# Up projections of two squared-ReLU MLPs: seven products of operand quarters in place of eight, in a one-core transformer kernel

## The chip, the cores and the metric

The kernel runs on 1 core of one Trainium2 chip. The metric is the device time of one execution in microseconds (us), as the median of several runs; lower is better. The core has TensorE (PE, matrix products; PEld is its weight load), VectorE (DVE), ScalarE (ACT), GpSimd (POOL) and SyncE (SP, which here only issues DMAs).

## The reference

Two transformer stacks over 512 tokens of width 1024, all in fp32. The first is one layer with attention, a memory cross-attention and a SwiGLU MLP. The second has two layers, each a mixer (mLSTM in the first, latent attention in the second) and then the MLP with which the change deals:

```python
ada = cond @ ada_w[l] + ada_b[l]                      # shift, scale and gate rows
sh1, sc1, g1, sh2, sc2, g2 = split(ada, 6)
x = x + g1 * rmsnorm(mixer(modulate(rmsnorm(x, norm_g[l, 0]), sh1, sc1)), norm_g[l, 1])
h = modulate(rmsnorm(x, norm_g[l, 2]), sh2, sc2)
y = square(relu(h @ mlp_w1[l])) @ mlp_w2[l]           # [512,1024] @ [1024,4096], @ [4096,1024]
x = x + g2 * rmsnorm(y, norm_g[l, 3])
```

## The kernel before

Every fp32 operand is held as two parts of 12 significant bits (`hi`, `lo`, type fp32r), and every product is three matmuls: hi by hi (L361), hi by lo (L362), lo by hi (L363), summed in PSUM (`ps`).

Weights stream from DRAM in chunks of 512 KB into `raw` (three buffers; L335 on SP's queue). A chunk is split into two parts, in pieces of 128x512: ACT copies the high part (L260), DVE subtracts it from the chunk for the low part (L261). Split chunks lie in the pool `s8` (14 buffers), which also holds the activations' parts. How many chunks may be split ahead is a cap (`w0` ... `w7`, `lc`). Where a weight has a gain by row, L270 and L271 do the same with the gain. `parts` (L481 ACT, L482 DVE) splits activations in the same way.

A squared-ReLU MLP has 4096 hidden columns, 32 hidden tiles of 128. They are worked in blocks (`mb`: 8, 6, 6, 6, 6 tiles). In a block, two tiles (a pair, 256 columns) at a time are made: per pair 2 tiles x 8 k-tiles x 3 = 48 matmuls of 128x512, then per tile a ReLU from PSUM on ACT (L1281), a square on DVE (L1283) and the split (L481, L482). Of the first block, the first two pairs (`fp`) are worked in two halves of 256 tokens, so that they can start while the layer's input is still being made. Then the block's down projection: for each half of the output columns and each of four token tiles the products over all k of the block in one bank; the first block is copied to an accumulator on ACT (L1184), later ones are added to it on DVE (L1186). The last block's down projection is woven with the step to the next layer (`boundary`).

A background generator (`ada`, `row_by`) makes the modulation rows of later layers: DVE multiplies a chunk of 256 KB of `ada_w` by a column of `cond` and adds it to an accumulator (L700, scalar_tensor_tensor 128x512). The chunks come by SP's queue (L704) into the tile `araw`, which has two buffers. A step is issued for each `pace` of matmul work; the steps run through the first of the two MLPs and end in the mixer behind it, so that the second MLP has none.

The kernel's instructions are written by generators and then put in order by a scheduler; each engine works its list strictly in that order. The list is fixed when the program is built.

The lines of the after kernel lie about 152 higher: L261 becomes L308, L482 L634, L700 L852, L704 L856, L1186 L1343, L361 to L363 L445 to L447.

Of the kernel before, what the change touches and what calls it, by code (L numbers as in the profile page):

```python
# [10 lines left out]
F32 = mybir.dt.float32  # L11
# [4 lines left out]
ALU = mybir.AluOpType  # L16
# [17 lines left out]
BUF = dict(s8=14, u2=16, row=3, raw=3, w0=4, w1=4, w2=4, w3=5, w4=5, w5=5, w6=5, w7=7, ps=8, pace=3, pacb=2.5, man=0, lag=3, lagx=3, lagm=3, half=1, quiet=1, xp=0, fp=2, r1=1.25, r1b=3.6, r1c=2.4, r2=1.6, r2b=2.6, rx=1.4, rm=0.6, pre=10, gl=3, pl=0, hb=300, hs=0, ha=0, sp=0, spq=1.3, sq=1, b1=1, b2=1, lc=7, mb=(8, 6, 6, 6, 6), mb2=(8, 6, 6, 6, 6), st2=1, pr2=8, z1=4.5, z2=5, gt=3, rv=2, gs=1, rl=3, n1=4, ex=2, em=3, vg=1, sb=(8, 8, 6), mo=4, x1=2, g0=20, st=1, y1=0, y2=1, y3=0, ph=2, pq=0, fy=1, u1=6, s32=4, sm=60)  # L34
# [19 lines left out]
class Nothing:  # L54
    """Stands for the core and its tiles while the order of the weights is drawn up."""
# [11 lines left out]
class HT:  # L67
    """A transposed operand [128, nk, ntok] as two exact parts, in tiles made when first used."""
# [36 lines left out]
class Net:  # L105
    def __init__(self, tc, args, out, dbg=None, specs=None, pools=None):
# [10 lines left out]
        self.n_lo = self.n_load = self.n_ready = self.n_take = 0  # L117
# [51 lines left out]
    def pump(self):  # L169
        """Loads and splits as far ahead as there is room for, in the order of use."""  # L170
# [3 lines left out]
        while more:  # L174
            more = False
            if self.n_load < len(self.specs) and self.raw_live < BUF["raw"]:
                i = self.n_load
                kk, cc, loader = self.specs[i][:3]
                self.raws[i] = self.t("raw", [P, kk, cc], F32, BUF["raw"])
                for f in self.before.pop(i, ()):  # L180
                    f()
                loader(self, self.raws[i])
                self.n_load += 1
                self.raw_live += 1
                more = True
            if self.n_ready < self.n_load:
# [13 lines left out]
    def piece(self):  # L200
        i, last, f = self.pieces.pop(0)
        f()
        if last:
            self.raw_live -= 1
            self.pump()
# [1598 lines left out]
```

## Time and profile before

| | |
|---|---|
| median of 3 runs | 2011.02 us (2007.4, 2011.02, 2011.51) |
| profiled execution, span | 2008.3 us |
| PE busy | 1961.0 us (98%) |
| DVE busy | 1256.9 us (63%) |
| ACT busy | 922.5 us (46%) |
| POOL busy | 311.5 us (16%) |

The profiled execution's own time is given by its span alone, and lies 2.7 us under the median. Busy shares are averages over stages. The first MLP's stretch from its sixth hidden tile to its last runs from 1112 to 1408 us of the span, the second's from 1672 to 1973 us.

### The profile page before, as it was taken

How to read it: one execution, taken by the hardware profiler on the slowest of the kernel's cores; microseconds unless marked ns; L12 is line 12 of the kernel's file. 1: busy time of each engine (PE TensorE's matmuls, PEld its weight loads, DVE VectorE, ACT ScalarE, POOL GpSimd, SP SyncE). 2: the span in 40 equal slices, each digit the busy share in tenths (PEclk: the TensorE clock that was granted, in tenths of full speed). 3: DMA queues.
4: the chain of work that ended last, by engine and by line, in shares of the span. 5: the costliest groups of instructions: out<-in, count | busy, mean ns of one | idle time of the engine just before them, and what ended most of it. 6: DMA issues, size and time to landing. Idle time of an engine off the chain costs nothing.

```text
span 2008.3 us, 27160 instructions
## 1 busy us (share of the span) xinstructions
PE 1961.0 (98%) x9652; PEld 1631.0 (81%) x9652; DVE 1256.9 (63%) x2379; ACT 922.5 (46%) x2073; POOL 311.5 (16%) x599
## 2 busy tenths in 40 slices
PE   8999999999999999999998999999999989999998
PEld 6888988878888888778887888888788878888886
DVE  5756655757558585757768557677777573444444
ACT  7767774645344243436534343233556543422331
POOL 1421113013100000511116000000420060000000
PEclk9999999999999999989999999999999999999999
DMA  6322342434446464244333455555341221422321
GB/s 209 92 80 77 114 136 64 143 100 126 148 152 206 138 213 139 69 136 140 118 116 108 144 163 184 169 185 177 111 132 43 85 74 53 128 95 93 95 84 42
DMA packets 191655, 244.98 MB, mean 122 GB/s; under 512 B 20059, under 2 KB 119488, under 8 KB 191520
## 3 DMA queue, kind: packets, MB, share of 16 engines
q1 hardware_dynamic: 185264, 232.15, 37.3%
q0 software_dynamic: 6256, 11.10, 2.1%
q8 instruction: 76, 1.25, 0.3%
q14 instruction: 59, 0.48, 0.1%
HBM read 241.00 MB, written 2.20 MB: 121 GB/s over the span
## 4 chain that ended last, share of the span: by engine, by line
PE 89%; DVE 6%; ACT 2%; issue 1%; DMA 1%; POOL 1%; SPq 0%; POOLq 0%; DVEq 0%; ACTq 0%
PE ps L361 26%; PE ps L362 26%; PE ps L363 26%; PE ps L859 1%; DVE s L271 1%; DVE x L502 1%; PE ps L1637 1%; DVE s L261 1%; PE ps L1666 1%; PE ps L1397 1%; PE ps L830 1%; PE ps L474 1%; PE ps L843 1%; PE ps L1143 1%; DVE s L482 1%
## 5 line engine op out<-in xcount | busy, mean ns | idle before, releaser
L361 PE MATMUL ps<-s,s 128*128 128x512 f32 (+3 forms) x2644 | 1016.2, 386 | 8.4 <-ACT s L481 7.5
L362 PE MATMUL ps<-s,s 128*128 128x512 f32 (+3 forms) x2644 | 1005.6, 381 | 9.0 <-DVE s L482 9.0
L363 PE MATMUL ps<-s,s 128*128 128x512 f32 (+3 forms) x2644 | 1001.9, 381 | 1.2 <-DVE s L482 1.2
L362 PEld LDWEIGHTS ps<-s,s 128*128 128x128 f32 (+1 forms) x2644 | 501.7, 190 | 104.9 <-DVE s L482 10.6
L361 PEld LDWEIGHTS ps<-s,s 128*128 128x128 f32 (+1 forms) x2644 | 500.0, 190 | 105.3 <-ACT s L481 10.3
L363 PEld LDWEIGHTS ps<-s,s 128*128 128x128 f32 (+1 forms) x2644 | 500.7, 190 | 101.2 <-DVE s L482 2.3
L260 ACT ACTIVATE s<-raw 128x512 fp32r<-128x512 f32 x359 | 205.5, 623 | 247.0 <-PE ps L363 183.8
L261 DVE TENSOR_TENSOR s<-raw,s 128x512 fp32r<-128x512 f32 x381 | 251.6, 702 | 94.5 <-ACT s L260 92.1
L700 DVE SCALAR_TENSOR_TENSOR u<-araw,cond,u 128x512 f32<-128x512 f32 x224 | 167.7, 749 | 132.5 <-DMA araw<-in_ada_w 105.7
L271 DVE SCALAR_TENSOR_TENSOR s<-raw,cols_all,s 128x256 fp32r<-128x256 f32 (+1 forms) x305 | 150.7, 546 | 14.3 <-ACT s L270 13.5
L270 ACT ACTIVATE s<-raw,cols_all 128x256 fp32r<-128x256 f32 (+1 forms) x283 | 134.8, 547 | 44.0 <-DMA raw<-in_w_gate_up 26.3
L416 POOL TENSOR_SCALAR sm<-sm 128x1 f32<-128x1 f32 x74 | 21.0, 284 | 601.3 <-ACT junk L427 598.3
L166 POOL DMA_DIRECT2D arow<-u x30 | 14.8, 494 | 636.3 <-DVE u L734 363.3
L481 ACT ACTIVATE s<-u 128x512 fp32r<-128x512 f32 x86 | 54.0, 628 | 113.6 <-DVE u L1283 62.2
L1186 DVE TENSOR_TENSOR u<-ps,u 128x512 f32<-128x512 f32 x80 | 54.2, 686 | 74.3 <-PE ps L363 73.8
L482 DVE TENSOR_TENSOR s<-ps,s 128x512 fp32r<-128x512 f32 (+3 forms) x124 | 74.5, 618 | 40.6 <-ACT s L481 40.2
L1281 ACT ACTIVATE u<-ps 128x512 f32<-128x512 f32 x64 | 38.0, 593 | 109.0 <-PE ps L363 107.9
L1283 DVE TENSOR_TENSOR u<-u 128x512 f32<-128x512 f32 x64 | 44.1, 689 | 66.4 <-ACT u L1281 65.9
L481 ACT ACTIVATE s<-ps 128x512 fp32r<-128x512 f32 (+3 forms) x124 | 64.5, 539 | 39.8 <-PE ps L474 22.9
L482 DVE TENSOR_TENSOR s<-u,s 128x512 fp32r<-128x512 f32 x86 | 58.9, 689 | 29.6 <-ACT s L481 26.5
L502 DVE SCALAR_TENSOR_TENSOR x<-u,sm,x 128x512 f32<-128x512 f32 x56 | 59.6, 1099 | 13.5 <-POOL sm L408 13.5
L408 POOL TENSOR_TENSOR sm<-sm,mhalf 128x1 f32<-128x1 f32 (+1 forms) x82 | 55.3, 674 | 52.6 <-DVE sm L1424 46.9
(241 smaller groups left out, 1741.0 us busy)
## 6 DMA issues: line engine op xcount, KB each, us to landing
raw<-in_mlp_w SPq DMA_DIRECT2D x128, 512.0 KB, 4.5
araw<-in_ada_w SPq DMA_DIRECT2D x192, 256.0 KB, 3.0
raw<-in_w_gate_up SPq DMA_DIRECT2D x44, 512.0 KB, 4.5
raw<-in_w_in SPq DMA_DIRECT2D x24, 512.0 KB, 4.1
raw<-in_a_w_in SPq DMA_DIRECT2D x24, 512.0 KB, 4.0
raw<-in_w_down SPq DMA_DIRECT2D x22, 512.0 KB, 3.7
raw<-in_w_mem_kv SPq DMA_DIRECT2D x16, 512.0 KB, 3.8
araw<-in_kv_ada_w SPq DMA_DIRECT2D x32, 256.0 KB, 2.9
```

Of the source, the lines that this page charges most:

```text
L260: A.activation(hi[:, sl, cl], src[:, sl, cl], AF.Copy)
L261: f.tensor_tensor(out=lo[:, sl, cl], in0=src[:, sl, cl], in1=hi[:, sl, cl].bitcast(F32), op=ALU.subtract)
L270: A.activation(hi[:, i, :], src[:, i, :], AF.Copy, scale=g)
L271: V.scalar_tensor_tensor(out=lo[:, i, :], in0=src[:, i, :], scalar=g, in1=hi[:, i, :].bitcast(F32), op0=ALU.mult, op1=ALU.subtract)
L361: self.nc.tensor.matmul(ps, lhsT=ah, rhs=bh, start=first and i == 0, stop=False)
L362: self.nc.tensor.matmul(ps, lhsT=ah, rhs=bl, start=False, stop=False)
L363: self.nc.tensor.matmul(ps, lhsT=al, rhs=bh, start=False, stop=last and i == n - 1)
L408: self.nc.gpsimd.tensor_tensor(out=r, in0=v, in1=self.mhalf[:, 0:n], op=ALU.pow)
L481: self.nc.scalar.activation(hi, x, AF.Copy)
L482: self.nc.vector.tensor_tensor(out=lo, in0=x, in1=hi.bitcast(F32), op=ALU.subtract)
L502: V.scalar_tensor_tensor(out=x, in0=y, scalar=r, in1=x, op0=ALU.mult, op1=ALU.add)
L700: V.scalar_tensor_tensor(out=acc, in0=raws.pop(j - 2), scalar=vec[:, j - 2:j - 1], in1=acc, op0=ALU.mult, op1=ALU.add)
```

## The change

1. Of 13 of each MLP's 16 pairs (blocks 1 to 4), the up projection is made as Strassen's product in Winograd's form: the weights' 1024x256 chunk pair and the input's 512x1024 are each cut into four quarters, and seven products of quarters (`wino`; 4 k-tiles x 3 matmuls of 128x256 each, L508) replace eight. Three PSUM banks of four take two products each. The sums of weight quarters are made anew for each pair (`split7`: seven ACT copies L341 and seven DVE subtractions L342 of 128x512 for seven parts, three DVE additions L345 and a scalar_tensor_tensor L361), the sums of input quarters once per MLP (`quarters`: 8 POOL additions, 8 DVE subtractions, 8 splits). The results are put together from PSUM by two ACT copies (L518, L528) and five DVE operations (L522, L524, L526, L530, L532) of 128x256.
2. The ReLU (L1438) and the square (L1439) are both on ACT.
3. The down projection of each block but the last runs over pairs of k-tiles outside, four token tiles (four banks) inside, and frees a weight chunk as soon as its k-tiles are done. This holds for the SwiGLU MLP as well.
4. `raw` has 4 buffers, the cap `w7` is 5, blocks are 6, 8, 6, 6, 6 with a cap per block (`mc`). The input lies in token halves (`HS`). All pairs of the first block are made in two halves of 256 tokens.

Numbers of instructions, before and after: PE matmuls 9300 and 10332; DVE tensor_tensor 1024 and 1252, scalar_tensor_tensor 956 and 1008; ACT activations 1820 and 2030; POOL tensor_tensor 106 and 122.

```diff
-BUF = dict(... raw=3, ... w7=7, ... mb=(8, 6, 6, 6, 6), mb2=(8, 6, 6, 6, 6), ...)
+BUF = dict(... raw=4, ... w7=5, ... mb=(6, 8, 6, 6, 6), mc=(4, 3, 4, 4, 4), ...)
...
+    def split7(self, c, p, raws):
+        A, V = self.nc.scalar, self.nc.vector
+        (b11, b12), (b21, b22) = ((r[:, :, 0:P], r[:, :, P:2 * P]) for r in raws)
+        both = self.big([P, 2, 2, 4, P], F32R)
+
+        def parts(j, x):
+            hi, lo = both[:, j, 0], both[:, j, 1]
+            A.activation(hi, x, AF.Copy)
+            V.tensor_tensor(out=lo, in0=x, in1=hi.bitcast(F32), op=ALU.subtract)
...
+        def third():
+            self.wsum = self.u2((P, 4, P))
+            add(self.wsum, b22, b12)
+            parts(1, self.wsum)
...
+    def wino(self, a, w, c):
...
+        def product(n, ps, first=True):
...
+            for k in range(4):
+                for e, (l, m) in enumerate(((wh, ah), (wh, al), (wl, ah))):
+                    nc.tensor.matmul(ps, lhsT=l[:, k, :], rhs=m[:, k, :], start=first and k == e == 0,
+                                     stop=k == 3 and e == 2, skip_group_check=True)
+                self.step(0.34)
+            if n % 2 or n == 6:
+                self.released()
...
+        product(0, p1)
+        m1 = half()
+        nc.scalar.activation(m1, p1, AF.Copy)
+        product(1, p3)
+        product(2, p6)
+        u = half()
+        V.tensor_tensor(out=u, in0=p6, in1=m1, op=ALU.subtract)
+        v = half()
+        V.tensor_tensor(out=v, in0=p3, in1=u, op=ALU.add)
+        product(3, p5)
+        V.tensor_tensor(out=y2[:, 256:S], in0=p5, in1=v, op=ALU.add)
+        product(4, p1, False)
+        nc.scalar.activation(y1[:, 0:256], p1, AF.Copy)
+        product(5, p3, False)
+        V.scalar_tensor_tensor(out=y1[:, 256:S], in0=p3, scalar=-1.0, in1=u, op0=ALU.mult, op1=ALU.subtract)
+        product(6, p5, False)
+        V.tensor_tensor(out=y2[:, 0:256], in0=p5, in1=u, op=ALU.add)
+        return y1, y2
...
-                    nc.scalar.activation(r, pss[i], AF.Relu)
-                    y = self.u2()
-                    V.tensor_tensor(out=y, in0=r, in1=r, op=ALU.mult)
+                    if k0:
+                        nc.scalar.activation(y, y, AF.Relu)
+                    nc.scalar.activation(y, y, AF.Square)
                     hi, lo = hid.k(m + i, ALL)
                     self.parts(hi, lo, y)
```

What this does to the order is seen at three places. The first is PE in the second MLP, in an up projection. Before, a pair's two banks follow one another, one matmul of 128x512 for each k-tile and part (`s8` first is the weights, second the input):

```order
L361 MATMUL ps_3239_16515<-s8_3101_15585,s8_3213_16297 128x512
L362 MATMUL ps_3239_16515<-s8_3102_15586,s8_3213_16297 128x512
L363 MATMUL ps_3239_16515<-s8_3101_15585,s8_3213_16297 128x512
L361 MATMUL ps_3239_16515<-s8_3101_15585,s8_3213_16297 128x512
L362 MATMUL ps_3239_16515<-s8_3102_15586,s8_3213_16297 128x512
L363 MATMUL ps_3239_16515<-s8_3101_15585,s8_3213_16297 128x512
```

After, each row is one product of twelve matmuls of 128x256:

```order
L508 MATMUL ps_3459_18635<-s8_3182_16426,s8_3448_18524 128x256 x12
L508 MATMUL ps_3460_18636<-s8_3267_16974,s8_3448_18524 128x256 x12
L508 MATMUL ps_3461_18637<-s8_3266_16973,s8_3454_18563 128x256 x12
L508 MATMUL ps_3462_18638<-s8_3265_16972,s8_3454_18563 128x256 x12
L508 MATMUL ps_3459_18635<-s8_3184_16434,s8_3455_18594 128x256 x12
L508 MATMUL ps_3477_18772<-s8_3182_16426,s8_3466_18667 128x256 x12
L508 MATMUL ps_3478_18773<-s8_3267_16974,s8_3466_18667 128x256
L508 MATMUL ps_3460_18636<-s8_3232_16635,s8_3455_18594 128x256 x12
L508 MATMUL ps_3462_18638<-s8_3268_16975,s8_3456_18624 128x256 x12
```

The next pair's first product (`ps_3477`) now stands between this pair's fifth and sixth; a pair takes four banks where it took two.

The second place is DVE in the first MLP, in the up projections of block 3 before (L1283 is the square, L482 the activation's low part, L261 a weight's, L700 the background):

```order
L1283 TENSOR_TENSOR u2_2354_12439<-u2_2353_12437 128x512
L482 TENSOR_TENSOR s8_2356_12442<-u2_2354_12439,s8_2355_12441 128x512
L261 TENSOR_TENSOR s8_2363_12497<-raw_2340_12350,s8_2363_12497 128x512 x2
L261 TENSOR_TENSOR s8_2366_12519<-raw_2350_12414,s8_2366_12519 128x512 x2
L1283 TENSOR_TENSOR u2_2358_12447<-u2_2357_12445 128x512
L261 TENSOR_TENSOR s8_2380_12592<-raw_2352_12435,s8_2380_12592 128x512 x2
L482 TENSOR_TENSOR u2_2361_12457<-u2_2331_12301,u2_2361_12457 64x512
L482 TENSOR_TENSOR s8_2356_12442<-u2_2358_12447,s8_2355_12441 128x512
L700 SCALAR_TENSOR_TENSOR u2_2365_12507<-araw_2374_12543,cond_880_4058,u2_2365_12507 128x512
```

After, in the up projections of the last block of the same MLP (`ps_2511`, `ps_2512`, `ps_2513` are a pair's banks, `araw` the background's chunks):

```order
L852 SCALAR_TENSOR_TENSOR u2_2501_13637<-araw_2504_13674,cond_881_4060,u2_2501_13637 128x512
L522 TENSOR_TENSOR u1_2521_13757<-ps_2512_13702,u1_2516_13718 128x256
L532 TENSOR_TENSOR u2_2492_13555<-ps_2490_13553,u1_2498_13607 128x256
L852 SCALAR_TENSOR_TENSOR u2_2501_13637<-araw_2517_13727,cond_881_4060,u2_2501_13637 128x512
L524 TENSOR_TENSOR u1_2522_13759<-ps_2511_13701,u1_2521_13757 128x256
L526 TENSOR_TENSOR u2_2515_13705<-ps_2513_13703,u1_2522_13759 128x256
L852 SCALAR_TENSOR_TENSOR u2_2501_13637<-araw_2518_13730,cond_881_4060,u2_2501_13637 128x512
L634 TENSOR_TENSOR s8_2509_13693<-u2_2491_13554,s8_2508_13692 128x512
L342 TENSOR_TENSOR s8_2519_13738<-raw_2485_13542,s8_2519_13738 128x512
L852 SCALAR_TENSOR_TENSOR u2_2501_13637<-araw_2523_13768,cond_881_4060,u2_2501_13637 128x512
L342 TENSOR_TENSOR s8_2519_13738<-u2_2520_13741,s8_2519_13738 128x512
L530 SCALAR_TENSOR_TENSOR u2_2514_13704<-ps_2511_13701,u1_2521_13757 128x256
```

The background's rows, which stood among work with slack, now stand between the rows that empty a pair's banks (L522 to L532) and those that make the next weights (L342).

The third place is DVE in the same MLP, at the down projection of block 3 after (L1343 adds a bank to the accumulator):

```order
L345 TENSOR_TENSOR raw_2451_13288<-raw_2451_13288 128x4x128
L852 SCALAR_TENSOR_TENSOR u2_2466_13399<-araw_2473_13429,cond_881_4060,u2_2466_13399 128x512
L634 TENSOR_TENSOR s8_2453_13295<-u2_2435_13154,s8_2453_13295 128x512
L852 SCALAR_TENSOR_TENSOR u2_2466_13399<-araw_2474_13431,cond_881_4060,u2_2466_13399 128x512
L882 COPY u2_2426_13124<-ps_2465_13383 1x512
L852 SCALAR_TENSOR_TENSOR u2_2466_13399<-araw_2475_13446,cond_881_4060,u2_2466_13399 128x512
L852 SCALAR_TENSOR_TENSOR u2_2466_13399<-araw_2476_13449,cond_881_4060,u2_2466_13399 128x512
L852 SCALAR_TENSOR_TENSOR u2_2466_13399<-araw_2478_13471,cond_881_4060,u2_2466_13399 128x512
L1343 TENSOR_TENSOR u2_2076_10751<-ps_2454_13302,u2_2076_10751 128x512
L1343 TENSOR_TENSOR u2_2078_10753<-ps_2455_13303,u2_2078_10753 128x512
```

Before, an add and two or more background rows alternate; after, the adds of four banks come together behind five background rows with two buffers.

## Rows read from the trace of the kernel before

**Rows 1.** The page: the span, busy time and share of each engine, and the chain that ended last.
```profile
span 2008.3 us, 27160 instructions
...
PE 1961.0 (98%) x9652; PEld 1631.0 (81%) x9652; DVE 1256.9 (63%) x2379; ACT 922.5 (46%) x2073; POOL 311.5 (16%) x599
...
PE 89%; DVE 6%; ACT 2%; issue 1%; DMA 1%; POOL 1%; SPq 0%; POOLq 0%; DVEq 0%; ACTq 0%
```

**Rows 2.** Busy time of each engine by stretch; the first line gives the columns. The first stretch is in the first squared-ReLU MLP, the other three in the second.
```profile
core 0: us, PE busy (x) PEld busy (x) DVE busy (x) ACT busy (x) POOL busy (x), PEclk, DMA share, GB/s
1112.00:1408.00 296.00, 296.00 (x1280) 239.42 (x1279) 199.46 (x309) 101.14 (x181) 20.15 (x40) 1.00 0.55 171
1672.00:1973.00 301.00, 301.00 (x1303) 244.25 (x1302) 118.33 (x184) 95.82 (x168) 0.00 (x0) 1.00 0.27 88
1807.00:1873.00 66.00, 66.00 (x287) 53.66 (x287) 28.09 (x44) 20.11 (x36) 0.00 (x0) 1.00 0.29 95
1873.00:1940.00 67.00, 67.00 (x291) 54.22 (x290) 28.28 (x44) 20.50 (x38) 0.00 (x0) 1.00 0.31 96
```

**Rows 3.** The same view for PE alone, in two stretches that hold matmuls of 128x256 only.
```profile
478.60:489.20 10.60, 10.60 (x92) 1.00 0.02 4
1657.00:1667.50 10.50, 10.50 (x92) 1.00 0.34 100
```

**Rows 4.** PE's list of instructions in time at the start of the second of those stretches (start us, us, instruction).
```profile
1657.08 0.28 PE L361 MATMUL ps<-s,s 128*128 128x256 f32 x1
1657.20 0.29 PE L362 MATMUL ps<-s,s 128*128 128x256 f32 x1
1657.32 0.28 PE L363 MATMUL ps<-s,s 128*128 128x256 f32 x1
1657.44 0.28 PE L361 MATMUL ps<-s,s 128*128 128x256 f32 x1
```

**Rows 5.** Groups of weight loads between 1657 and 1667.5 us (count | busy us, mean ns of one | idle before).
```profile
L363 PEld LDWEIGHTS ps<-s,s 128*128 128x128 f32 x32 | 6.0, 188 | 0.0
```

**Rows 6.** Groups of DVE's instructions in the first MLP, 1112 to 1408 us (count | busy us, mean ns of one | idle time before them and what ended it).
```profile
L261 DVE TENSOR_TENSOR s<-raw,s 128x512 fp32r<-128x512 f32 x106 | 68.3, 685 | 10.7 <-ACT s L260 10.2
L700 DVE SCALAR_TENSOR_TENSOR u<-araw,cond,u 128x512 f32<-128x512 f32 x82 | 61.5, 749 | 54.4 <-DMA araw<-in_ada_w 48.4 <-DMA u<-in_ada_b 5.1
L1283 DVE TENSOR_TENSOR u<-u 128x512 f32<-128x512 f32 x26 | 17.9, 687 | 5.0 <-ACT u L1281 4.5
L1186 DVE TENSOR_TENSOR u<-ps,u 128x512 f32<-128x512 f32 x24 | 16.2, 684 | 1.2 <-PE ps L363 1.1
```

**Rows 7.** DVE's waits in the same stretch: who waits for what, us in total, times, the longest.
```profile
DVE u L700 <- DMA araw<-in_ada_w: 48.4, 38, 4.1
```

**Rows 8.** DVE's list of instructions in time in the first MLP (start us, us of the run, instruction, in brackets the idle time before and what ended it).
```profile
1207.59 1.29 DVE L261 TENSOR_TENSOR s<-raw,s 128x512 fp32r<-128x512 f32 x2
1209.12 1.54 DVE L700 SCALAR_TENSOR_TENSOR u<-araw,cond,u 128x512 f32<-128x512 f32 x2 [0.24 <-DMA araw<-in_ada_w]
1210.58 0.69 DVE L1283 TENSOR_TENSOR u<-u 128x512 f32<-128x512 f32 x1
1211.18 1.28 DVE L261 TENSOR_TENSOR s<-raw,s 128x512 fp32r<-128x512 f32 x2
1212.38 0.68 DVE L482 TENSOR_TENSOR s<-u,s 128x512 fp32r<-128x512 f32 x1
1213.70 1.54 DVE L700 SCALAR_TENSOR_TENSOR u<-araw,cond,u 128x512 f32<-128x512 f32 x2 [0.64 <-DMA araw<-in_ada_w]
```

**Rows 9.** DVE in the same stretch, where runs follow one another without a gap.
```profile
1224.17 1.29 DVE L261 TENSOR_TENSOR s<-raw,s 128x512 fp32r<-128x512 f32 x2
1225.85 0.75 DVE L700 SCALAR_TENSOR_TENSOR u<-araw,cond,u 128x512 f32<-128x512 f32 x1 [0.39 <-DMA araw<-in_ada_w]
1226.52 1.29 DVE L261 TENSOR_TENSOR s<-raw,s 128x512 fp32r<-128x512 f32 x2
1227.72 0.68 DVE L1186 TENSOR_TENSOR u<-ps,u 128x512 f32<-128x512 f32 x1
```

**Rows 10.** SP's issues of the background's chunks at that place (start us, us, x issues), and from the page the DMA groups (xcount, KB each, us from issue to landing).
```profile
1209.90 1.11 SPq L704 DMA_DIRECT2D araw<-in_ada_w  x2
...
araw<-in_ada_w SPq DMA_DIRECT2D x192, 256.0 KB, 3.0
```

**Rows 11.** Groups of DVE and ACT instructions over the whole span: narrow ones, a wide STT from three tiles, and a square.
```profile
L864 DVE TENSOR_TENSOR s<-ps,sm 128x256 f32<-128x256 f32 x16 | 6.8, 423 | 20.6 <-PE ps L859 20.4
L271 DVE SCALAR_TENSOR_TENSOR s<-raw,cols_all,s 128x256 fp32r<-128x256 f32 x240 | 104.4, 491 | 8.4 <-ACT s L270 7.7
...
L1400 ACT ACTIVATE s<-ps 128x256 f32<-128x256 f32 x16 | 6.1, 383 | 9.4 <-PE ps L1397 9.3
L1419 ACT ACTIVATE u<-s 128x512 f32<-128x512 f32 x8 | 5.0, 622 | 0.0
```

**Rows 12.** Groups of POOL and DVE over the whole span: additions of 128x512 on POOL, and DVE's instructions in the stretches where POOL works.
```profile
L457 POOL TENSOR_TENSOR u<-u,row 128x512 f32<-128x512 f32 x12 | 16.6, 1382 | 1.7 <-ACT u L456 1.7
L464 DVE TENSOR_TENSOR u<-u,row 128x512 f32<-128x512 f32 x12 | 12.1, 1004 | 0.1
```

More of the change, by code (lines that the diff above doesn't have):

```diff
@@ L98, in __init__, with add, get @@
         self.net, self.k, self.ends = net, [], {}
+    def add(self, i, n):
+        have = []
+        def get(j):
+            if not have:
+                have.append(self.net.got(i, 0))
+            hi, lo = have[0]
+            return hi[:, j, :], lo[:, j, :]
+        self.k += [lambda j=j: get(j) for j in range(n)]
+        self.ends[len(self.k) - 1] = True
     def used(self, k):
@@ L175, in pump @@
             more = False
-            if self.n_load < len(self.specs) and self.raw_live < BUF["raw"]:
+            if self.n_load < len(self.specs):
                 i = self.n_load
[L178 to L184, printed above, removed]
-                more = True
@@ L186, in pump @@
[L186 to L198 removed]
+                kk, cc, loaders = self.specs[i][:3]
@@ L340, in loader @@
                         net.nc.sync.dma_start(out=dst, in_=src)
-            hi, lo = self.take(n, cn, loader, gain and (gain, k))
-            for i in range(n):
-                g.k.append((hi[:, i, :], lo[:, i, :]))
-            g.ends[len(g.k) - 1] = True
+            g.add(self.take(n, cn, (loader,), gain and (gain, k)), n)
         return g
@@ L359, in prod @@
         n = len(pairs)
-        for i, ((ah, al), (bh, bl)) in enumerate(pairs):
+        for i, pair in enumerate(pairs):
+            (ah, al), (bh, bl) = (x() if callable(x) else x for x in pair)
             self.nc.tensor.matmul(ps, lhsT=ah, rhs=bh, start=first and i == 0, stop=False)
@@ L1164, in cross, with mlp @@
         return ho
-    def mlp(self, blocks, up, w_down, g, nxt, first, ready=None, both=False):
+    def mlp(self, blocks, up, w_down, g, nxt, first, ready=None, caps=None):
         nc, V = self.nc, self.nc.vector
@@ L1173, in mlp @@
             hid = HT(self, nb)
+            if caps:
+                self.cap(caps[b], True)
             up(k0, nb, hid)
@@ L1192, in part @@
                 return ms
-            if last and both:
+            if last:
                 self.cap(BUF["lc"], True)
@@ L1320, in mlstm @@
         wg = Group(self)
-        hi, lo = self.take(KD, 64, loader)
-        wg.k = [(hi[:, k, :], lo[:, k, :]) for k in range(KD)]
-        wg.ends[KD - 1] = True
+        wg.add(self.take(KD, 64, (loader,)), KD)
         psg = self.bank()
```

195 lines of the change are left out of this document (140 added, 55 removed).

## The prediction, made before the changed kernel had run

> **What bounds the kernel now.** First the page: PE is busy 98% of the span and holds 89% of the chain that ended last [rows 1]. So time is gained by taking matmul work from PE, wherever PE has nothing else to wait for. Next the stretches of the two MLPs: PE is busy in each microsecond of both, at a granted clock of 1.00, that is at 2.4 GHz; DVE is busy 199 of 296 us in the first and 118 of 301 us in the second [rows 2]. The difference is the background: 82 rows of L700 for 61.5 us, and before them 54.4 us in which DVE stood still, nearly all for a chunk in `araw` [rows 6, 7]. DVE works its list in order, so everything behind an L700 waits too. Today that costs nothing, since PE has work ahead. DVE's busy time and those waits together are 199.5 + 54.4 = 254 of 296 us: the first MLP has about 40 us of room on DVE, the second some 180.
>
> **Durations.** DVE's operations overlap at their ends, so I count from start to start: 128x512 takes 0.60 us (1210.58, 1211.18, two rows, 1212.38), not the 0.69 shown [rows 8]; an L700 0.67 (1225.85 to 1226.52) [rows 9]. For 128x256 the group shows 423 ns [rows 11]; less the same overlap of 0.085 it is 0.34. L530 has three operands, two of them tiles; its nearest rows lie between 423 and 491 ns [rows 11], so 0.34 to 0.41; I take 0.34, and 26 of them are worth under 2 us either way.
>
> **PE.** Between 1807 and 1940 us 578 matmuls of 128x512 took 133 us, 0.230 us each [rows 2]. In the two stretches of 128x256 alone 184 took 21.1 us, 0.115; the starts lie 0.12 apart [rows 3, 4]. Some records of matmuls may be missing or cut at a border, so I take 0.231 and 0.118. A pair's up projection goes from 48 x 0.231 = 11.07 to 84 x 0.118 = 9.89 us. That is 1.18 us for each of 26 pairs, 30.7 us in all, 15.4 for each MLP. The one pair more of each first block that is made in halves costs 96 x 0.118 - 48 x 0.231 = 0.2 us. These gains hold if a weight load stays hidden at 128x256: one lasts 188 ns in the records [rows 5], more than the 118 of spacing, and yet the spacing is 118, so loads lie beside one another and beside matmuls. Where half the columns follow each load, that was already so in the rows that I used.
>
> A rule of the Trainium skill speaks against this. The page "TensorE: Matmul & The Clock Gate" gives a weight load of 128 columns as 128 / 1.2 = 107 ns (section "LDWEIGHTS (loading the stationary operand)"), and says under "The mechanism" that a load overlaps matmuls in flight only where its group of rows differs. All loads here use the full array. An estimate from the page's formulas without overlap: 84 x (107 + 109) = 18.1 us for a pair after and 48 x (107 + 216) = 15.5 before, so the change would cost some 68 us. The trace does not agree: 118 ns from start to start has no room for 107 + 109.
>
> **Squares, ACT and POOL.** ACT takes over the squares (622 ns [rows 11]) and per pair three more copies of weights and two of 128x256 (383 ns [rows 11]): (3 + 2) x 0.62 + 2 x 0.38 = 3.9 us, 51 us for 13 pairs on top of 101 of 296 [rows 2]. It stays far from being the bound, at nothing. POOL's eight additions of input quarters last 1.4 us each [rows 12], 11 us, under the first block's down projection of 33 us (144 matmuls). DVE beside POOL is slower, 1.00 us for 0.69 [rows 12]: at most 16 operations x 0.3 = 5 us, at least nothing. I take 1 us.
>
> **DVE in the second MLP.** By DVE's list after, the span from one pair's first combination (L522) to the next has some 15 us less than PE's around a down projection, and at its densest holds 9.6 us (6 L342, 4 L308, an L345, L361 and L634, five combinations) beside PE's 9.89. Nothing waits for `araw`. It holds, with handoffs: DVE empties a bank only after PE is done with it, and four banks of eight belong to a pair, so I let 2 of the 15.4 us go (between 0 and 6).
>
> **DVE in the first MLP.** Here it does not hold. From the first combination of block 1 to the last of block 4 DVE's list after holds 91 L342, 83 L852, 52 L308, 45 L634, 39 L345, 24 L1343, 13 L361, 65 combinations and a few small ones: at 0.60, 0.67 and 0.34, 253 us. PE has 273 in the same stretch. To this come the waits for `araw`. Two buffers are filled anew only when the row before has read them: a chunk that was issued at 1209.90 was used at 1213.70 [rows 8, 10], and the landing alone has a median of 3.0 us [rows 10]. So a row cannot start sooner than some 3.5 us after the end of the second one before it. With that rule, walking through the list, before has 56 us of waits (54.4 were measured [rows 6]), after 34 us; with 3.0 it would be 40 and 22, with 4.0 72 and 46. I take 3.5, which fits. DVE then needs 253 + 34 = 287 us where PE needs 273 and took 289 before: DVE is the bound, and the 15.4 us are gone but for 2.
>
> It is worse where the work is not even. By block, DVE's work and waits against PE's in the same piece of both lists:
> Block 1, three pairs to the start of the down projection: 33 x 0.60 + 15 x 0.67 (some narrower) + 15 x 0.34 = 34, with waits 37.0, against 3 x 9.89 = 29.7: 7.3 over.
> Block 2, to the first add (L1343): 37 x 0.60 + 17 x 0.67 + 13 x 0.34 = 38.0, with 8.3 of waits 46.3, against 39.3: 7.0 over, of which PE covers half by doing 20 matmuls of the down projection ahead of the last pair's two final products: 3.5.
> Block 3: 36.0 + 6.6 against 39.3: 3.3 over.
> Block 4, two pairs: 27 x 0.60 + 10 x 0.67 + 11 x 0.34 = 26.6, with 2.9, against 21.2: 8.3 over.
> In the down projections between, DVE has 3 to 12 us to spare; it catches up there, but it can't work ahead, since caps of 3 and 4 chunks stop the splitting. The sum is 22 us in which PE waits. This is where the order shows L852 between L522 and L524, and five L852 with two buffers ahead of the four adds: those five hold the banks of the down projection for some two round trips. For handoffs at the blocks' ends I add 2 us.
>
> **Sum.** First MLP: -15.4 + 22.4 + 2 + 1 = +10. Second: -15.4 + 2 = -13.4. Halves +0.4. The new order of the down projections costs PE nothing and the SwiGLU MLP was not waiting: 0. The smaller cap before the boundaries is put at 0 (it can cost 2). Together -3: against the profiled 2008.3 that is 2005, and as the median of the runs lies 2.7 above that execution, 2008.
>
> **Rivals.** (a) The waits in the first MLP are shorter than I count: with a round trip of 3.0 us DVE needs 253 + 22 = 275, PE's 273, and the blocks' overhang shrinks to some 10 us. For it: the landing's median is 3.0 [rows 10], and chunks are asked for earlier where DVE has other work between. Against: 3.5 gives the measured waits of before. It would be 2008 - 12 = 1996; if nothing at all is lost, 1981. It decides if the overhang is below 10 us. (b) On the other side: two-buffer waits get worse, as the first MLP's `raw` chunks, now asked for two at a time, stand ahead of the background's on SP's queue. With 4.0 the waits are 46, 12 more, nearly all of it in blocks that are over already; with 4.1, the longest today [rows 7], for each of the rows at a block's critical place, 20 more. That is 2020 to 2030; slower from an overhang of 29 us on. For it: DMA is busy 55% in this stretch [rows 2], and PE's stop halts the background's pace as well. (c) In the second MLP DVE's chain from bank to bank (9.6 beside 9.89) doesn't hold: half the gain is lost there, 2015. (d) Weight loads are not hidden where products change banks, and the change doesn't save anything on PE: then both lose, 2040 and more; the rows against it are above.
>
> **How the numbers follow.** Chances: as forecast (2002 to 2014) 0.38; (a) 0.27; (b) and (c) together 0.33; (d) 0.02. I forecast 2008. The range reaches from the middle of (a) to the upper end of (b), 1992 to 2028; the likeliest case alone is 2002 to 2014. A measurement of this kernel tells 0.2% from no change, 4 us: faster is below 2007, slower above 2015. Faster takes (a) and near half of the forecast case, 0.43; the same 0.23; slower 0.34.
>
> **What would show it.** After, the second MLP's PE should be busy throughout and its stretch 13 us shorter; the matmuls L508 0.118 us apart. The first MLP should show PE idle for some 25 us, waiting for DVE's L342 and L522 to L532 and for L1343, and DVE without idle time but for `araw`, some 34 us of it. I am wrong if PE has under 10 us of idle time there (a), if the waits for `araw` exceed 45 us (b), or if PE waits in the second MLP for more than 5 us (c).

## The result, and the profile after

The changed kernel takes 2033.92 us, against 2010.32 us for the kernel before on the same chip: a ratio of 1.0121 with a 95% interval of 1.0107 to 1.0136. It is 23.6 us slower. The prediction said 2008, in a range of 1992 to 2028: a fall of 3 us was forecast, the time rose, and it lies 6 us above the range.

The page of the profile after, its span, its engines and its chain:

```profile
span 2031.5 us, 29708 instructions
...
PE 1941.8 (96%) x10684; PEld 1665.1 (82%) x10684; DVE 1396.7 (69%) x2659; ACT 1025.0 (50%) x2283; POOL 331.7 (16%) x615
...
PE 69%; DVE 14%; issue 6%; DMA 5%; ACT 4%; POOL 2%; DVEq 0%; POOLq 0%; ACTq 0%
```

Against [rows 1] PE is busy 19.2 us less, and yet the span is 23.2 us longer: 42.4 us of new idle time on PE. Its share of the chain fell from 89% to 69%; DVE (6 to 14%), issue (1 to 6%) and DMA (1 to 5%) took most of it over. The mean granted clock went from 0.989 to 0.982. PE's waits over the whole span, after (who waits for what: us in total, times, the longest):

```profile
PE ps L869 <- DVE u L634: 17.0, 4, 6.4
PE ps L446 <- DVE s L634: 11.9, 7, 3.3
PE ps L508 <- DVE u L524: 6.9, 3, 5.8
```

The first line is nearly new: L869 (L717 before, where PE waited 0.9 us for it in all) is the matmul that sums a finished background row over the partitions. It stands in PE's list in order, and everything on PE stands behind it.

To see where the time went I cut each profiled execution at the same instructions: the first gate activation of the SwiGLU, the first modulated tile of the mLSTM layer, of the first squared-ReLU MLP and of the second, and the first norm behind the first MLP. The table is worked out from the starts of these instructions in the traces, in us; each column is the time from one to the next, the first from the start and the sixth to the end, and the span is their sum. "Latent" is the latent attention between the two MLPs. The spans are those of the profiled executions, which lie 0.6 to 5.2 us under the medians of their kernels (in e1 0.1 above), so that differences of a few us between two rows can be those of two executions. e1 to e12 are the experiments below.

| kernel | to SwiGLU | SwiGLU | mLSTM | MLP 1 | latent | MLP 2 | span |
|---|---|---|---|---|---|---|---|
| before | 481.5 | 338.3 | 236.7 | 369.3 | 195.9 | 386.6 | 2008.3 |
| changed | 493.1 | 337.1 | 233.0 | 388.5 | 207.3 | 372.5 | 2031.5 |
| e1 second MLP alone | 492.2 | 337.1 | 234.4 | 370.2 | 200.3 | 372.4 | 2006.6 |
| e2 same, raw 3 | 480.2 | 338.2 | 236.2 | 369.8 | 198.3 | 371.7 | 1994.4 |
| e3 changed, one chunk | 493.1 | 337.1 | 232.9 | 374.4 | 198.4 | 372.0 | 2007.9 |
| e4 changed, row sum late | 495.7 | 336.6 | 235.5 | 396.9 | 254.2 | 402.3 | 2121.2 |
| e5 before, raw 4 | 491.7 | 337.3 | 232.5 | 369.2 | 199.9 | 388.7 | 2019.3 |
| e6 changed, raw 3 | 481.2 | 338.2 | 235.2 | 381.0 | 207.4 | 372.5 | 2015.5 |
| e7 e6, araw 4 | 483.2 | 338.1 | 236.6 | 371.9 | 194.4 | 371.6 | 1995.8 |
| e8 e7, pace 2.2 | 483.5 | 339.0 | 236.1 | 364.4 | 188.7 | 374.4 | 1986.1 |
| e9 before, araw 4, pace 2.2 | 483.8 | 338.9 | 236.3 | 369.1 | 193.0 | 387.7 | 2008.8 |
| e10 e2, araw 4, pace 2.2 | 482.5 | 339.1 | 236.2 | 368.0 | 194.0 | 372.6 | 1992.4 |
| e11 e7, pace 1.7 | 484.9 | 347.3 | 236.3 | 360.3 | 191.5 | 372.1 | 1992.4 |
| e12 e2, squares on DVE | 481.5 | 338.1 | 235.2 | 369.8 | 195.6 | 373.1 | 1993.3 |

So the change lost 11.6 us ahead of the SwiGLU (4.9 of it came back in the SwiGLU and the mLSTM), 19.2 in the first MLP and 11.4 in the latent attention, and won 14.1 in the second MLP.

The cut behind the first MLP does not divide the same work in each kernel, since the first norm falls at another place of the last down projection. Counted in the traces without the row sums, the first MLP and the latent attention hold 1419 and 457 matmuls of 128x512 before, 758 and 446 in the changed kernel, 776 and 428 in e3, 759 and 445 in e6, 775 and 429 in e7, 772 and 432 in e8, 770 and 434 in e11. The sum falls by 672 each time, which is 14 pairs of 48, so 747 in the first MLP would be the cut of before. At 0.231 us each, 2.5 us of the first MLP's 388.5 in the changed kernel, 6.7 in e3, 2.8 in e6, 6.5 in e7, 5.8 in e8 and 5.3 in e11 are work that lies in the latent attention before. Below, "at equal work" stands for times that are corrected by it: the changed kernel lost 16.7 us in the first MLP and 13.9 in the latent attention.

The second MLP went as written. The stretch after (columns as in [rows 2]) and the group of its new matmuls between 1700 and 2031 us:

```profile
1659.00:2031.50 372.50, 356.66 (x2226) 319.71 (x2224) 247.86 (x403) 178.34 (x342) 45.48 (x53) 0.99 0.29 91
```
```profile
L508 PE MATMUL ps<-s,s 128*128 128x256 f32 x1092 | 130.5, 280 | 0.0
```

1092 matmuls of 128x256 with no idle time before them; 130.5 us of busy time for 13 pairs of 84, 0.1195 each. Against that the first MLP: DVE's wait for chunks and PE's waits, 1117 to 1430 us.

```profile
DVE u L852 <- DMA araw<-in_ada_w: 26.2, 21, 2.3
...
PE ps L869 <- DVE u L634: 10.6, 3, 5.2
PE ps L508 <- DVE u L524: 6.9, 3, 5.8
```

The largest of these waits is in block 4, where the prediction had put its 8.3 us. DVE's list there (start us, us of the run, instruction):

```profile
1413.17 0.75 DVE L852 SCALAR_TENSOR_TENSOR u<-araw,cond,u 128x512 f32<-128x512 f32 x1
1413.83 0.42 DVE L532 TENSOR_TENSOR u<-ps,u 128x256 f32<-128x256 f32 x1
...
1414.77 0.75 DVE L852 SCALAR_TENSOR_TENSOR u<-araw,cond,u 128x512 f32<-128x512 f32 x1
...
1420.06 1.29 DVE L308 TENSOR_TENSOR s<-raw,s 128x512 fp32r<-128x512 f32 x2
1421.27 0.42 DVE L522 TENSOR_TENSOR u<-ps,u 128x256 f32<-128x256 f32 x1
...
1425.21 0.42 DVE L524 TENSOR_TENSOR u<-ps,u 128x256 f32<-128x256 f32 x1
```

DVE runs here almost without a gap, background rows, next weights and combinations in turn, and L524 has read the bank p3 at 1425.6; PE had stood for it since 1420.0 (5.77 us before its L508 at 1425.78).

What a wait costs beyond itself is seen behind the longest one, in the latent attention: PE's list in time, and two stretches before and after 1517 us.

```profile
1517.10 0.79 PE L869 MATMUL ps<-u,onesr 128*128 128x512 f32 x1 [6.44 <-DVE u L634]
...
1518.76 0.63 PE L446 MATMUL ps<-s,s 128*128 128x512 f32 x1
1519.19 0.63 PE L447 MATMUL ps<-s,s 128*128 128x512 f32 x1
1519.62 0.63 PE L445 MATMUL ps<-s,s 128*128 128x512 f32 x1
```
```profile
1506.00:1517.00 11.00, 4.67 (x26) 4.02 (x25) 7.39 (x14) 2.93 (x8) 1.31 (x3) 0.95 0.50 142
1517.00:1530.00 13.00, 12.90 (x51) 10.49 (x52) 8.30 (x17) 6.71 (x13) 3.33 (x8) 0.78 0.42 128
```

After standing for 6.4 us PE's matmuls of 128x512 start 0.43 us apart, where it was 0.23: that is the lower level of the clock, 1.2 GHz, and it shows as a granted 0.78 over the next 13 us. From 1522.7 us on, after 5.6 us without a wait, the starts are 0.23 apart again. The Trainium skill, page "TensorE: Matmul & The Clock Gate", section "What's actually happening", says that the slow clock is the resting state and activity releases it; the trace agrees. In the first MLP after (1123 to 1451 us), 48 starts of matmuls lie more than one and a half times the median apart without a gap between them, 7.4 us beyond the median in all; before there is none in its 1116 to 1426.

One more thing is seen on DVE just ahead of this stretch, while POOL makes its eight additions of input quarters (L480). Three background rows on DVE take 12.19 us in all; the second of them alone is recorded from 1114.56 to 1125.18, 10.62 us in place of 0.75:

```profile
1113.78 12.19 DVE L852 SCALAR_TENSOR_TENSOR u<-araw,cond,u 128x512 f32<-128x512 f32 x3
1114.55 10.07 POOL L480 TENSOR_TENSOR u<-s 128x512 f32<-128x512 f32 x8
...
1138.42 0.79 PE L869 MATMUL ps<-u,onesr 128*128 128x512 f32 x1 [5.21 <-DVE u L634]
```

The same stands in e8 (10.74 us) and e11 (10.77); in e3, e6 and e7, where the additions take 13 us, most of the DVE instructions beside them last 1.65 to 1.8 us. The last line is the longest wait of PE for a row sum in the first MLP, and that row is the one that DVE was working on.

### The profile page after: what moved, and what is told of

Same layout as the page of the kernel before. It is cut to its first block, busy times and chain, and to the rows that moved or that the text cites. A ratio compares the mean times of both kernels' runs of the same rounds, so it can differ in the third digit from the quotient of the medians.

```text
span 2031.5 us, 29708 instructions
## 1 busy us (share of the span) xinstructions
PE 1941.8 (96%) x10684; PEld 1665.1 (82%) x10684; DVE 1396.7 (69%) x2659; ACT 1025.0 (50%) x2283; POOL 331.7 (16%) x615
## 4 chain that ended last, share of the span: by engine, by line
PE 69%; DVE 14%; issue 6%; DMA 5%; ACT 4%; POOL 2%; DVEq 0%; POOLq 0%; ACTq 0%
PE ps L447 18%; PE ps L446 18%; PE ps L445 18%; PE ps L508 7%; DMA araw<-in_ada_w 3%; DVE u L852 2%; DVE s L308 2%; DVE s L318 2%; PE ps L1011 1%; DVE s L634 1%; DVE s L342 1%; DVE x L654 1%; ACT junk L579 1%; PE ps L1793 1%; PE ps L1822 1%
## 5 line engine op out<-in xcount | busy, mean ns | idle before, releaser
L445 PE MATMUL ps<-s,s 128*128 128x512 f32 (+4 forms) x2260 | 857.8, 383 | 8.4 <-ACT s L633 4.8
L446 PE MATMUL ps<-s,s 128*128 128x512 f32 (+4 forms) x2260 | 850.5, 377 | 12.2 <-DVE s L634 11.9
L447 PE MATMUL ps<-s,s 128*128 128x512 f32 (+4 forms) x2260 | 845.2, 377 | 4.7 <-DVE s L634 4.6
L446 PEld LDWEIGHTS ps<-s,s 128*128 128x128 f32 (+1 forms) x2260 | 431.7, 191 | 90.0 <-DVE s L634 13.7
L447 PEld LDWEIGHTS ps<-s,s 128*128 128x128 f32 (+1 forms) x2260 | 430.2, 190 | 86.7 <-DVE s L634 7.4
L445 PEld LDWEIGHTS ps<-s,s 128*128 128x128 f32 (+1 forms) x2260 | 429.7, 191 | 84.9 <-ACT s L633 7.5
L508 PE MATMUL ps<-s,s 128*128 128x256 f32 x2184 | 265.3, 282 | 10.0 <-DVE u L524 6.9
L508 PEld LDWEIGHTS ps<-s,s 128*128 128x128 f32 x2184 | 262.8, 189 | 13.8 <-issue 5.9
L852 DVE SCALAR_TENSOR_TENSOR u<-araw,cond,u 128x512 f32<-128x512 f32 x224 | 177.2, 791 | 108.6 <-DMA araw<-in_ada_w 87.2
L308 DVE TENSOR_TENSOR s<-raw,s 128x512 fp32r<-128x512 f32 x277 | 193.3, 736 | 42.5 <-ACT s L307 37.0
L317 ACT ACTIVATE s<-raw,cols_all 128x256 fp32r<-128x256 f32 (+1 forms) x283 | 134.2, 547 | 47.5 <-issue 22.1
L634 DVE TENSOR_TENSOR s<-ps,s 128x512 fp32r<-128x512 f32 (+3 forms) x124 | 75.2, 619 | 40.6 <-ACT s L633 39.7
L341 ACT ACTIVATE s<-raw 128x512 fp32r<-128x512 f32 x104 | 62.6, 621 | 67.9 <-PE ps L447 32.9
L634 DVE TENSOR_TENSOR s<-u,s 128x512 fp32r<-128x512 f32 x102 | 69.7, 686 | 39.4 <-ACT s L633 35.8
L633 ACT ACTIVATE s<-u 128x512 fp32r<-128x512 f32 x102 | 63.6, 625 | 64.0 <-DVE u L1403 49.3
L341 ACT ACTIVATE s<-u 128x512 fp32r<-128x512 f32 x78 | 48.7, 624 | 61.0 <-DVE u L345 31.6
L342 DVE TENSOR_TENSOR s<-raw,s 128x512 fp32r<-128x512 f32 x104 | 70.5, 682 | 11.0 <-ACT s L341 10.9
```

The costliest lines, as they stand in the source:

```text
L308: f.tensor_tensor(out=lo[:, sl, cl], in0=src[:, sl, cl], in1=hi[:, sl, cl].bitcast(F32), op=ALU.subtract)
L317: A.activation(hi[:, i, :], src[:, i, :], AF.Copy, scale=g)
L341: A.activation(hi, x, AF.Copy)
L445: self.nc.tensor.matmul(ps, lhsT=ah, rhs=bh, start=first and i == 0, stop=False)
L446: self.nc.tensor.matmul(ps, lhsT=ah, rhs=bl, start=False, stop=False)
L447: self.nc.tensor.matmul(ps, lhsT=al, rhs=bh, start=False, stop=last and i == n - 1)
```

## The experiments

**e1 and e2: the first MLP as before, and three raw buffers.** The edits to the changed kernel, e2 with the last line as well:

```diff
-                if k0:
+                if k0 and l:
                     ys = self.wino(quarters, w, (k0 + m) * P)
...
-        for i, tok in enumerate((slice(0, 256), slice(256, S))):
+        toks = (slice(0, 256), slice(256, S)) if halves or isinstance(h, HS) else (ALL,)
+        for i, tok in enumerate(toks):
...
-        self.mlp(BUF['mb'], ..., BUF['mc'])
+        self.mlp(BUF['mb'], ..., BUF['mc'] if l else None)
...
-        hn = HS(self, KD)
+        hn = HT(self, KD)
...
-BUF = dict(... raw=4, ...)
+BUF = dict(... raw=3, ...)
```

The first MLP's caps per block and its input in token halves go back with it.

> The changed kernel with the seven products in the second squared-ReLU MLP alone; the first MLP's up projections are eight products over 512 tokens as before (its blocks, its squares on ScalarE and the new order of its down projections stay). The theory that the first MLP loses more than it gains, because the vector engine (its work, and its standing for the background's chunks) makes PE wait and the clock fall: the first MLP's stretch, 335 us after the change, goes back to about 310, the mixer behind it loses its extra wait of 6 us for a background row, and the time falls from 2033.9 to about 2002 to 2006. Rival, that the second MLP gains nothing either and the losses lie in what all stages share (buffers, caps): 2020 or more.

Measured: 2006.48 us, ratio 0.9982 (0.9973 to 0.9991). The first MLP is back at 370.2 us (310.2 of them from 60 us after its start on, where the changed kernel has 328.5), with no idle time of PE from 1101 to 1408 us, and the second keeps its 372.4. So the blocks, the squares on ScalarE and the new order of the down projections, which stay, cost the first MLP 0.9 us here, and 0.5 in e2.

> As the run before, with three buffers for raw weights as in the kernel before in place of four. The stages ahead of the first MLP came 7 us later after the change though nothing in them was changed by name. Theory that the fourth buffer does this (weights are asked for earlier and stand ahead of other loads on SP's queue): those 7 us come back, about 6 us under the run before. Rival, that it is the order of the SwiGLU's down projections or the cap: the same time as the run before, within 2 us, or longer, since a pair of the second MLP takes two of the three buffers.

Measured: 1996.36 us, 0.9931 (0.9916 to 0.9946): 10 us under e1, and the 12 us ahead of the SwiGLU are back. One place where they were lost is seen on ScalarE in the boundary ahead of the cross attention. e1, with four buffers (L317 is the high part of a weight, L579 the square sum of a norm, L598 the norm of a tile):

```profile
329.05 0.63 ACT L579 ACTIVATE junk<-x 128x512 bf16<-128x512 f32 x1 [0.28 <-DVE x L654]
...
329.68 2.50 ACT L317 ACTIVATE s<-raw,cols_all 128x256 fp32r<-128x256 f32 x6
332.08 0.61 ACT L579 ACTIVATE junk<-x 128x512 bf16<-128x512 f32 x1
...
334.62 0.72 ACT L598 ACTIVATE u<-x,sm 128x512 f32<-128x512 f32 x1 [0.31 <-POOL sm L560]
```

and e2, with three:

```profile
327.61 0.63 ACT L579 ACTIVATE junk<-x 128x512 bf16<-128x512 f32 x1 [0.29 <-DVE x L654]
...
328.24 1.70 ACT L317 ACTIVATE s<-raw,cols_all 128x256 fp32r<-128x256 f32 x4
329.85 0.61 ACT L579 ACTIVATE junk<-x 128x512 bf16<-128x512 f32 x1
...
332.18 0.73 ACT L598 ACTIVATE u<-x,sm 128x512 f32<-128x512 f32 x1
```

With one more raw buffer more weights are there, and six pieces of them instead of four stand in the list ahead of the last token tile's norm: from the first L579 shown to L598 it is 5.57 us in place of 4.57. The boundary ahead of the SwiGLU has the same once more, 8 pieces and 5.21 us in place of 6 and 4.22. PE has 11.9 us of idle time from 318 to 500 us in e1, and 6.1 in e2 from 316 to 490, and its clock is 0.91 and 0.96 in the first 40 us. I had expected SP's queue as the way. ScalarE's list is one way, but these two places make 2 of the 12 us. By the starts of L598, e1 is 1.5 us behind e2 ahead of the first of these boundaries, 2.5 at the row shown, 4.6 at the next tile, and in the second boundary 7.1, 8.1 and 10.7; at the last tile of each, ScalarE stands for DVE's L654 longer than in e2. How that follows from the buffer was not shown.

**e5: the fourth raw buffer alone, in the kernel before** (`raw=3` to `raw=4`, nothing else).

> The kernel before with four buffers for raw weights in place of three and nothing else. If the fourth buffer alone slows the boundaries between the early stages (splits of weights stand ahead of the norm of the next token tile on ScalarE), the time goes up by 6 to 10 us, to 2017 to 2021, and the stage from the first boundary to the cross attention's end is 7 us longer. Rival: it does so only with the new caps and the new order of the down projections: within 3 us of 2011.

Measured: 2023.38 us, 1.0067 (1.0050 to 1.0084), 2 us above what was expected; 10.2 us more ahead of the SwiGLU. The fourth buffer costs that with none of the other edits.

**e6: the changed kernel with three raw buffers.**

> The changed kernel with three buffers for raw weights. By the fourth buffer's cost in the early stages alone: 2033.9 - 8 to 10 = 2024 to 2026. Rival: the first MLP, whose pairs take two raw buffers at once, gets worse with three, and the gain is eaten: 2032 or more.

Measured: 2020.67 us, 1.0047 (1.0032 to 1.0062), 13 us less than the changed kernel. In the profiled executions it is 16.0: 11.9 ahead of the SwiGLU less 3.3 behind it, and 7.5 in the first MLP (381.0), which I had not expected to gain; why it does was not shown. What stays of the loss is 11.7 us in the first MLP and 11.5 in the latent attention, at equal work 8.9 and 14.3.

**e3: the background without its chunks' waits.**

```diff
-                    raws[j] = self.t("araw", [P, n], F32, 2)
-                    nc.sync.dma_start(out=raws[j], in_=ws[:, j, :])
+                    if n == S and b is not None:
+                        if self.araw1 is None:
+                            self.araw1 = self.t("araw1", [P, n], F32, 1)
+                            nc.sync.dma_start(out=self.araw1, in_=ws[:, j, :])
+                        raws[j] = self.araw1
+                    else:
+                        raws[j] = self.t("araw", [P, n], F32, 1)
+                        nc.sync.dma_start(out=raws[j], in_=ws[:, j, :])
```

The few narrower rows still load their chunks, into one buffer.

> The changed kernel, with the background's rows all computed from one chunk that is loaded once: the vector engine does every multiplication as before, but never waits for a chunk (the modulation rows are then not those of the reference, and 50 MB less are loaded). Theory that the waits for chunks make the first MLP's loss: PE's idle time there falls from 24 us to under 8, with it the low clock, and the time from 2033.9 to about 2005 to 2012. Rival, that the vector engine's work alone is too much in the up projections: over 15 us of PE's idle time stay, 2025 or more.

Measured: 2009.90 us, 24 us less than the changed kernel. PE's idle time from 1098 to 1409 us is 10.1 us (24.8 from 1098 to 1428 after), a little over the 8 that was expected. The first MLP takes 14.1 us less, the latent attention 8.9; at equal work 18.3 and 4.7. DVE's group of background rows there, and PE's largest wait in the stage (L853, L876 and L635 here are L852, L869 and L634 after):

```profile
L853 DVE SCALAR_TENSOR_TENSOR u<-araw,cond,u 128x512 f32<-128x512 f32 x80 | 66.0, 825 | 0.8
```
```profile
PE ps L876 <- DVE u L635: 5.2, 3, 3.8
```

As many rows as in the changed kernel, no wait for chunks, and PE's waits for the row sums are halved with it. The rival, that DVE's work alone is too much, falls as the main cause; but the stage is still 5 us longer than before, at equal work 1.6 shorter, where PE has 15 us less to do. This run also takes load off DMA (a busy share of 0.31 in place of 0.51); e7 leaves that as it is.

**e4: the row sum later in PE's list** (`y2=1` to `y2=4`).

> The changed kernel, with the matmul that sums a background row over partitions (L869) written four background steps after its operand is made in place of one. PE's own list has it in order, and PE waited 17 us there. Theory that this one place in PE's list is the cost: the 17 us and the low clock behind them go, 2033.9 falls to about 2012 to 2018. Rival, that the vector engine is late in any case and PE waits elsewhere instead (for the combinations, the weights' parts): 2028 or more.

Measured: 2123.10 us, 1.0566 (1.0547 to 1.0585). It tells nothing of the one place: three more background steps for each of 30 row sums, at a step per 2.5 to 3 us of matmul work, delayed all rows. The last row sum came at 1793 us in place of 1548, and layers waited for their modulation:

```profile
PE ps L869 <- DVE u L634: 89.9, 6, 22.1
```

**e7 and e8: four buffers for the background's chunks, and more of it earlier.** To e6:

```diff
-                    raws[j] = self.t("araw", [P, n], F32, 2)
+                    raws[j] = self.t("araw", [P, n], F32, 4)
...
-BUF = dict(... pace=3, ...)
+BUF = dict(... pace=2.2, ...)
```

(The last two lines are e8's; the run before, for e7, is e6.)

> As the run before, with four buffers for the background's chunks in place of two (the freed space). If the waits for those chunks in the vector engine's list make the first MLP's loss, its stretch falls from 388 to about 374 us, the mixer's wait for a background row goes too, and the time is 2024 - 14 - 9 = about 2000. If DMA itself is the limit there (bandwidth, queue order) and not the two buffers, it stays above 2015.

Measured: 1999.45 us, 0.9942 (0.9928 to 0.9957), 21 us under e6: 9.1 in the first MLP and 13.0 in the latent attention, at equal work 12.8 and 9.3. DVE's wait for chunks in the first MLP:

```profile
DVE u L852 <- DMA araw<-in_ada_w: 1.0, 2, 0.7
```

24.9 us of it in e6, 1.0 here, with the same chunks loaded over the same queue and the same DMA share (0.49 and 0.50): the two buffers were the limit, not DMA.

> As the run before, with the background's steps written every 2.2 us of matmul work in place of 3 in the stages ahead of the first MLP, so that about a third more of its rows is done there. If the vector engine's work in the first MLP is what is left of the loss, its stretch falls further, to 360 to 368 us, and the time to 1985 to 1995. Rival: the earlier stages then wait for the background as the first MLP did: 2005 or more.

Measured: 1986.68 us, 0.9882 (0.9867 to 0.9897). This is the fastest version, 1.2% under the kernel before. The first MLP and the stage up to 1544 us:

```profile
1058.60:1423.00 364.40, 353.18 (x2197) 315.94 (x2196) 314.97 (x496) 182.68 (x348) 60.58 (x87) 0.99 0.46 144
1423.00:1544.20 121.20, 117.28 (x672) 104.14 (x671) 88.49 (x227) 74.98 (x186) 27.11 (x49) 0.99 0.29 84
```

DVE still is busy 315 of 364 us. In the first MLP stand 72 background rows (87 in the changed kernel, 95 before), in the latent attention none up to 1544 us, where the changed kernel had 16 and the kernel before 8.

**e9 and e10: controls.** The same two edits in the kernel before, and in e2.

> The kernel before with four buffers for the background's chunks and the pace of 2.2: the control for the run of 1986.7 us. PE had nothing to wait for in the first MLP before, so there the two edits should give nothing (369 us, within 1); the mixer behind it may give 2 to 7 us, since fewer rows are left for it. 2004 to 2009. Rival, that most of the gain of 1986.7 comes from the background alone: under 2000.

Measured: 2010.94 us, 0.9998 (0.9988 to 1.0007). The first MLP is as expected (369.1) and the latent attention gives 2.9 us, but the stages ahead of the first MLP take 2.5 more, and the time lies 2 us above what was expected. Without the seven products the background's buffers and pace are worth nothing that can be measured.

> Seven products in the second MLP alone, three raw buffers, four chunk buffers and the pace of 2.2. If seven products in the first MLP now give something (its stretch was 364.4 us), this run's first MLP takes 369 to 370 and the time is about 1991, 5 us above the run with both; if they still give nothing, 1985 or less.

Measured: 1994.29 us, 0.9918 (0.9901 to 0.9934). So seven products in the first MLP are now worth some 7 us (7.6 by the medians, 6.3 in the profiled executions), half of their 15.4: 3.6 us in the MLP and 5.3 behind it; 1.8 are given back in the second. The 5.3 are the cut again: e8 has 24 matmuls of 128x512 fewer in the latent attention than e10, 5.5 us. The time is 3 us above the 1991 that was expected.

**e11: the pace 1.7.**

> Seven products in both, three raw buffers, four chunk buffers, the pace 1.7 in place of 2.2: another third of the background's rows comes ahead of the first MLP. If the vector engine's remaining background rows still cost there, 364 goes to about 358 and the time to 1978 to 1982; if what is left is the clock behind short waits and the blocks' own unevenness, the first MLP stays at 362 to 365 and the time within 3 us of 1986.7; if the earlier stages begin to wait for background rows, above 1992.

Measured: 1994.16 us, 0.9920 (0.9905 to 0.9935). The first MLP falls to 360.3 us with 16 background rows left in it, between my first two cases, and the third came with it: the SwiGLU, which now holds 126 rows in place of 95 in e8, goes from 339 to 347.

**e12: the squares back on DVE** in both MLPs, in e2.

> The second run (seven products in the second MLP alone, three raw buffers, 1996.4 us) with the squares on the vector engine, as before. The vector engine has some 0.3 us of room for each pair in the second MLP by the prediction's count, and a pair's two squares are 1.2 us: if the place of the squares matters, the second MLP's 372 us go up by 4 to 12. If not, 1996.4 within 2.

Measured: 1995.33 us, 0.9925 (0.9910 to 0.9940), as e2. The place of the squares doesn't matter in the second MLP. Its stage is 1.4 us longer in the profile, within what two executions differ by.

## Why the prediction was wrong

**The step that failed: what the sum put at nothing.** Outside the two MLPs the sum has 0: "The new order of the down projections costs PE nothing", "The smaller cap before the boundaries is put at 0"; the fourth raw buffer and the background's leftovers behind the first MLP have no term at all. Stage by stage (forecast, then measured in the profiled executions): ahead of the first MLP 0 and +6.7; first MLP +10 and +19.2; latent attention 0 and +11.4; second MLP -13.4 and -14.1; the halves +0.4, which lie in the MLPs. The 26 us between the forecast -3 and the measured +23.2 are 11.4 in the latent attention, 9.2 in the first MLP and 6.7 ahead of it, less 1.1.

**The fourth raw buffer: never priced.** By e5 it costs 10.2 us ahead of the SwiGLU in a kernel with nothing else changed, and by e6 13 us in the whole in the changed kernel, with 7.5 in the first MLP of the profiled executions. The prediction's sum for the first MLP, +10, stands beside +11.7 in e6, at equal work +8.9, where raw is as before.

**The stage behind: not in the sum.** The background is written by the pace of matmul work. A pair's steps count 28 x 0.34 = 9.5 in place of 16 x 0.65 = 10.4, so 13 pairs move the background 11 us of pace later, some four steps of two chunks. 16 of its rows, not 8, came into the latent attention, where nothing covers them: PE waited 6.4 us in one piece for one row sum, and the stage lost 11.4 us. With four chunk buffers (e7) its 16 rows are still there and 9.3 of the 14.3 us at equal work in e6 are gone: most of it was the waits. The other 5.0 are not explained.

**DVE in the first MLP: right for block 4, and in size by luck.** The sum said 22 us of PE's waiting plus 2; measured 24.0 us of idle time from 1123 to 1451 us. But I had given it to the combinations and adds of four blocks: 7.3, 3.5, 3.3 and 8.3. Without the waits for row sums the blocks have 4.5, 0, 0.7 and 8.2 (block 4: 0.87 + 1.60 + 5.77). The other 10.6 us are PE's waiting for row sums (L869), which I had not put on PE's list at all: I had followed what a late background row does to DVE's queue, and not that PE has an instruction of the background's in order too. The waits for chunks were 26.2 us for the 34 predicted; by the prediction's own walk that is a round trip between 3.0 us (22) and 3.5 (34). Nor was DVE without idle time but for chunks: it stood still 52 us from 1123 to 1452, 26.2 of them for chunks. That the waits for chunks are the main cause is shown by e3 and e7: without them the stage takes 14.1 and 9.1 us less, at equal work 18.3 and 12.8.

**DVE beside POOL: too small.** The term was 1 us, at most 16 operations x 0.3. The 1.00 us of [rows 12] is a mean over twelve L464 that took 0.68 to 1.79 us, with more or less of POOL's work beside them; after the change one L852 took 10.62. How much of PE's wait of 5.21 us behind it comes from this and how much from the chunks, no run separates.

**The clock: no term.** I counted idle time one for one. What came on top was 7.4 us of slow matmuls in the first MLP, and more behind it. With it the sum there comes out: at equal work the first MLP takes 16.7 us more where the matmuls alone take 15.2 less, 31.9 in all; in the whole stage PE's idle time went up by 24.0 (from 7.1 to 31.0) and the time lost in slow starts by 7.0 (from 2.6 to 9.6).

**PE's work: right.** 84 x 0.118 in place of 48 x 0.231 us. The second MLP was put at -13.4 and measured -14.1. The starts of 128x256 matmuls lie 118 ns apart after, as [rows 3, 4] had it, so the weight loads stay hidden and rival (d) falls.

**The rivals.** The result lies beyond the range of (b), which named slower waits for chunks as the way. They were not slower but faster than I had counted, so (b) was not right either: the right side for another reason. (c) fell: the second MLP has 5.3 us of PE's waiting for DVE, all of it in its first 40 us, at the boundary, and the stage won what was forecast; the sign that I had set for (c), more than 5 us of waiting there, was set too low, since the same stage has 5.5 us of idle time on PE before the change as well.

What stays open: why the fourth buffer costs what it does beyond ScalarE's two places, why it costs in the first MLP, and the 5.0 us in the latent attention. Of the first MLP's 15 us, e8 shows 5 and e11 9; at equal work it is 10.7 and 14.3. What e8 still lacks, 4.5 us, is covered by PE's idle time (11.2 us, 7.1 in the kernel before) and slow starts (4.0 us, 2.6 before). The new order of the down projections was not tried alone: SwiGLU, where it stands by itself, is 0.1 us shorter in e2 than before, and the first MLP, where e2 has it too, 0.5 longer.

## What to carry to other kernels

When work is moved from an engine that is full to one that has room, count the room by stage and with what else stands in that engine's list in order, waits included: here the same edit won 14 us beside a vector engine with room and lost 12 (e6) beside a background job with two buffers. A background job that is paced by the main work moves when the main work gets shorter; look for where its leftovers land, and for its instructions on every engine. Price each buffer count and cap as a change of its own, with a run of the old kernel: one buffer more cost 10 us. Before times of two stages are compared, count the work on either side of the cut between them.

## What was not expected of the hardware

Matmuls behind a wait ran at half speed: behind the one of 6.4 us a granted 0.78 over 13 us is 0.22 x 13 = 2.9 us more, nearly half as much again. Two more buffers for 256 KB chunks took DVE's waits from 24.9 us to 1.0 over the same queue at a DMA share of 0.5. One instruction of DVE took 10.62 us in place of 0.75 while POOL made eight additions in a row.
